# A chunked RWKV-7 recurrence on one core: ScalarE makes the block operand's copy of the state and the modified keys' factor

## The chip, the core and the metric

One NeuronCore of a Trainium2 chip runs the whole program. TensorE (PE in the rows) does the matrix products, VectorE (DVE), ScalarE (ACT) and GpSimd (POOL) work on tiles in on-chip memory, and SyncE (SP) issues the DMAs. Each engine takes its instructions in the order in which they are written for it, and waits on semaphores for the others. The metric is the device time of one execution in microseconds.

## The reference

Two layers of a diffusion trunk are computed for 128 context tokens and 512 latent tokens together (640 rows). A layer is a modulated norm, one projection, four mixers (RWKV-7, latent attention, gMLP, a Fourier mixer) and an output projection. The change lies in the RWKV-7 mixer, which scans the tokens in both directions with a state of 8 heads x 64 x 64:

```python
ah = heads(jax.nn.sigmoid(p['rwkv_a0'][d] + ad @ p['rwkv_a_up'][d]))
kt = kh * (1.0 + (ah - 1.0) * k_a)
...
def step(S, inp):
    r_t, w_t, k_t, v_t, kk_t, a_t = inp
    sa = jnp.einsum('bhvk,bhk->bhv', S, -kk_t)
    S = (S * w_t[:, :, None, :] + sa[..., None] * (kk_t * a_t)[:, :, None, :]
         + v_t[..., None] * k_t[:, :, None, :])
    return S, jnp.einsum('bhvk,bhk->bhv', S, r_t)
```

`kt` are the modified keys; the carried state is S.

## The kernel before, in words

The scan is done in chunks of 64 tokens. A *job* is one chunk in one direction: 2 + 8 chunks times 2 directions, 20 jobs in each of the two layers. `recurrence` holds two generators for a job. `intra` makes everything of a chunk that does not need the carried state: decays (L730 on ScalarE, the scan L732 on VectorE, the exponentials L737 and L739 on ScalarE), the modified keys `kt` (L745, L746), the operands `Ks` and `Qs` (L752 to L757), their products (L765 on TensorE), masked by L768 into `GG`, and then the inverse of a triangular 64 x 64 block by five doubling levels, each a product (L815), a masked copy (L816), two products (L822, L823) and an addition (L826). L831 and L832 follow on TensorE when the last level has been added; L834, L838 and L841 end it. `chain` carries the state through: it copies the state into the block operand `ZZ` (L851, L852), and goes on with L855, L857, L862, L863 and L864, L868, the new state (L870, L871), and the output (L876, L878). Up to four `intra` and two `chain` generators are advanced in turn.

Beside them runs `fill`, dense projections of 128x320 tiles (L168 to L170) that need nothing of the recurrence, evacuated by L355, L374 and L375. Their weights are split by L144 and L145. So TensorE's program is a mixture of small products and groups of six or twelve dense ones.

The order of instructions on an engine is set when the program is built, by a scheduler with costs of its own; taking instructions off an engine may shift others. The two half tiles of `ZZ` (one for each head of a pair, in `HALF[0]` = partitions 0 to 63 and `HALF[1]` = 64 to 127) are filled from the state before L855 and again from R before L868. `p["kah"]` holds half of k_a for each partition, four columns, and `tha` is the tanh from which ah follows as (tha + 1) / 2.

Of the kernel before, what the change touches and what calls it, by code (L numbers as in the profile page):

```python
# [8 lines left out]
F32 = mybir.dt.float32  # L9
F32R = mybir.dt.float32r  # L10
F16 = mybir.dt.float16
AF = mybir.ActivationFunctionType
ALU = mybir.AluOpType
# [43 lines left out]
def trunk(ctx: ExitStack, tc: tile.TileContext, A: dict, O: dict, dbg: dict):  # L57
    nc = tc.nc
    mm = nc.tensor.matmul
    V, S_, G = nc.vector, nc.scalar, nc.gpsimd  # L60

    cst = ctx.enter_context(tc.tile_pool(name="cst", bufs=1))
    lay = ctx.enter_context(tc.tile_pool(name="lay", bufs=2))
# [14 lines left out]
    def bank1():  # L78
        return cur["m"].tile([128, 512], F32, tag="m1", name="m1")
# [136 lines left out]
    def layer_params(l):  # L216
        vec = lay.tile([128, NV], F32, tag="vec", name="vec")
        nc.sync.dma_start(vec, A["vec"][l])

        def g(n):  # L220
            o, c = VEC[n]
            return vec[:, o:o + c]
        p = {n: g(n) for n in VEC}
        d = lay.tile([128, 14 + 14 + 4 + 4 + 32 + 16], F32, tag="der", name="der")
        V.tensor_scalar(d[:, 0:14], p["mu"], -1.0, 1.0, op0=ALU.mult, op1=ALU.add)
        V.tensor_scalar_mul(d[:, 14:28], p["mu"], 0.5)
        V.tensor_scalar_mul(d[:, 28:32], p["kk"], -0.5)
        V.tensor_scalar_mul(d[:, 32:36], p["ka"], 0.5)
        V.tensor_scalar_mul(d[:, 36:68], p["bm"], 0.5)
        V.tensor_scalar_mul(d[:, 68:84], p["wa0"], 0.5)  # L230
        p["omu"], p["hmu"], p["kkn"], p["kah"], p["bmh"], p["wah"] = (
            d[:, 0:14], d[:, 14:28], d[:, 28:32], d[:, 32:36], d[:, 36:68], d[:, 68:84])
        p["mod"] = lay.tile([128, 24, 2], F32, tag="mod", name="mod")
        lp[l] = p
# [109 lines left out]
    def layer(l, X, h, w13):  # L344
        p = lp[l]
# [338 lines left out]
        def recurrence(y):  # L684
            with tc.tile_pool(name=f"rw{l}", bufs=1) as rw:
                units = [(u, j) for u in range(4) for j in range(2)]
                HALF = (slice(0, 64), slice(64, 128))

                def t1k(name, shape=(128, 4, 64), dt=F32):
                    return rw.tile(list(shape), dt, tag="t1", name=name, bufs=8)  # L690

                def keep(name, shape, dt=F32, bufs=3):
                    return rw.tile([128] + list(shape), dt, tag="k" + name, name=name, bufs=bufs)
# [8 lines left out]
                def b3(ps):  # L702
                    return ps[:, 0:256].rearrange("p (a t) -> p a t", t=64)
# [4 lines left out]
                def intra(seg, i, d, A16, XZ):  # L708
# [13 lines left out]
                    def inp(kind):  # L722
                        a = rk[:, 4 * kind:4 * kind + 4, 64 * (ch % 2):64 * (ch % 2) + 64]
                        return a if d == 0 else a[:, :, ::-1]

                    th = th[:, :, 64 * (i % 2):64 * (i % 2) + 64]
                    thw, tha = th[:, 0:4, :], th[:, 4:8, :]
# [14 lines left out]
                    Pi, Pe = P[:, :, 1:65], P[:, :, 0:64]  # L742

                    kt = t1k("kt")
                    V.scalar_tensor_tensor(kt, tha, -1.0, p["kah"][:, 0:4, None].to_broadcast([128, 4, 64]), op0=ALU.add, op1=ALU.mult)  # L745
                    V.scalar_tensor_tensor(kt, kt, 1.0, inp(1), op0=ALU.add, op1=ALU.mult)  # L746
                    yield


# [50 lines left out]
                    for lev in range(1, 6):  # L800
                        if lev == 2:

                            ZZ = keep("ZZ", (2, 4, 64))
# [44 lines left out]

                def chain(it, d, St):
                    Qs, ZZ, GK, GR, Z1, KT, PC, ch, first = it  # L850
                    V.tensor_copy(ZZ[0:64, 0], St[0:64])  # L851
                    S_.copy(ZZ[64:128, 1], St[64:128])  # L852
                    ps = bank1()
                    for u, j in units:
                        mm(ps[HALF[j], 64 * u:64 * u + 64], GK[:, j, u, :], ZZ[:, j, u, :], start=True, stop=True)  # L855
                    R = t1k("R")
                    S_.copy(R, b3(ps))  # L857
                    yield
                    ps = bank1()
                    for u, j in units:  # L860
                        rr = HALF[j]
                        mm(ps[rr, 64 * u:64 * u + 64], Z1[rr, u, :], R[rr, u, :], start=True, stop=True)  # L862
                    V.tensor_copy(ZZ[0:64, 0], b3(ps)[0:64])  # L863
                    S_.copy(ZZ[64:128, 1], b3(ps)[64:128])  # L864
                    yield
                    ps = bank1()
                    for u, j in units:
                        mm(ps[HALF[j], 64 * u:64 * u + 64], KT[:, u, j, :], ZZ[:, j, u, :], start=True, stop=True)  # L868
                    Sn = rw.tile([128, 4, 64], F32, tag="S", name="S", bufs=4)
                    V.tensor_add(Sn, St, b3(ps))  # L870
                    V.tensor_mul(Sn, Sn, PC[:, :, None].to_broadcast([128, 4, 64]))  # L871
                    yield
                    ps = bank1()
                    for u, j in units:
                        rr = HALF[j]
                        mm(ps[rr, 64 * u:64 * u + 64], St[rr, u, :], Qs[rr, u, 1, :], start=(u == 0), stop=False, skip_group_check=True)  # L876
                    for u, j in units:
                        mm(ps[HALF[j], 64 * u:64 * u + 64], ZZ[:, j, u, :], GR[:, j, u, :], start=False, stop=(u == 3), skip_group_check=True)  # L878
                    dst = y[:, :, 64 * ch:64 * ch + 64]
                    if d == 1:  # L880
                        dst = dst[:, :, ::-1]
                    if first:
                        S_.copy(dst, b3(ps))
                    else:
                        V.tensor_add(dst, dst, b3(ps))
                    return Sn
# [6 lines left out]
                while order or active or chains or jobs:  # L893
                    if jobs and len(active) < nact and since >= STAG:
                        jb = jobs.pop(0)
                        active.append((jb, intra(*jb, A16s[count % 3], XZs[count % 3])))
                        count += 1
                        since = 0
                    since += 1

                    if order and len(chains) < 2 and order[0] in done and not any(c[0][0] == order[0][0] and c[0][2] == order[0][2] for c in chains):
                        s_, i, d = jb = order.pop(0)
                        if i == 0:
                            t = rw.tile([128, 4, 64], F32, tag="S", name="S0", bufs=4)
                            if s_ == 0:
                                G.memset(t, 0.0)
                            else:
                                nc.sync.dma_start(t, A["state"][l, :, 4 * d:4 * d + 4, :])
                            state[s_, d] = t
                        chains.append((jb, chain(done.pop(jb), d, state[s_, d])))  # L910
                    running = len(chains) + len(active)
                    for lst in (chains, active):
                        for e in list(lst):
                            try:
# [3 lines left out]
                                s_, i, d = e[0]  # L918
# [341 lines left out]
        if l + 1 < L:  # L1260
            layer_params(l + 1)
# [127 lines left out]
    load_x(X, HALVES[0])  # L1389
    nc.sync.dma_start(con, A["consts"])  # L1390
    layer_params(0)
    V.tensor_copy(c16, i64)
    V.tensor_copy(blk_r, blk)
# [162 lines left out]
```

## Time and profile before

| | |
|---|---|
| median of 3 runs | 2326.18 us (2321.11 to 2326.68) |
| the profiled execution | 2325.5 us, its span 2323.7 us, so 1.8 us lie around the span |
| TensorE busy | 2180.2 us, 94% of the span |
| VectorE busy | 1448.5 us, 62% |
| ScalarE busy | 1103.1 us, 47% |
| GpSimd busy | 890.2 us, 38% |
| mean granted TensorE clock | 0.98 |

Busy shares are means over stages with different limits: the two recurrences (about 370 to 700 us, and 1525 to 1870 us) have to be read by themselves. Times inside the execution are microseconds from the start of the span.

### The profile page before, as it was taken

To read this page: it belongs to the slowest core of one execution; us is meant where nothing else is said; L and a number is where in the kernel's file an instruction comes from. 1 tells how busy PE (TensorE), PEld (TensorE's weight loads), DVE (VectorE), ACT (ScalarE), POOL (GpSimd) and SP (SyncE) were. 2 spreads that over 40 slices of the span, in tenths; PEclk is the share of its full clock that TensorE was granted. 3 is DMA by queue.
4 is the path that set the end of the run, shared out by engine and by line. 5 is a ranking of instruction groups with operands and counts; after the bars stand their busy time and mean duration, and the time that the engine had idled before them with its cause. 6 is when DMAs were issued, how large, how long until landed. Compare 5 with 4: busy or idle time off the path is not lost. (4 is left out here: it accounts for less than half of the span.)

```text
span 2323.7 us, 49631 instructions
## 1 busy us (share of the span) xinstructions
PE 2180.2 (94%) x19662; PEld 2014.1 (87%) x19662; DVE 1448.5 (62%) x2816; ACT 1103.1 (47%) x2399; POOL 890.2 (38%) x892
## 2 busy tenths in 40 slices
PE   6899998999999999899999999989999999998998
PEld 4888897888889999878998888978888899997997
DVE  5677757888874326822366787578889643367225
ACT  5666754444434334423345766544444343344332
POOL 2322125443443335523552222244444334355452
PEclk8999999999999999999999999999999999999999
DMA  7233326332215426565532323362322254264332
GB/s 262 73 100 91 108 88 203 101 91 95 78 58 176 150 74 191 150 226 191 153 96 83 106 80 100 113 198 88 97 87 72 63 178 152 76 187 147 95 106 99
DMA packets 208010, 283.74 MB, mean 122 GB/s; under 512 B 26912, under 2 KB 119712, under 8 KB 207776
## 3 DMA queue, kind: packets, MB, share of 16 engines
q1 hardware_dynamic: 207776, 280.55, 38.8%
q8 instruction: 155, 2.54, 0.5%
q14 instruction: 79, 0.65, 0.1%
HBM read 224.75 MB, written 55.74 MB: 121 GB/s over the span
## 5 line engine op out<-in xcount | busy, mean ns | idle before, releaser
L145 POOL TENSOR_TENSOR wl<-wr,wh 128x512 fp32r<-128x512 f32 x371 | 523.1, 1413 | 966.3 <-ACT wh L144 853.0
L168 PE MATMUL dps<-hhi,wh 128*128 128x320 f32 x2368 | 772.1, 326 | 8.7 <-DVE f L1150 4.2
L169 PE MATMUL dps<-hlo,wh 128*128 128x320 f32 x2368 | 743.6, 314 | 5.9 <-POOL hlo L306 4.6
L170 PE MATMUL dps<-hhi,wl 128*128 128x320 f32 x2368 | 741.3, 313 | 0.0
L168 PEld LDWEIGHTS dps<-hhi,wh 128*128 128x128 f32 x2368 | 452.2, 191 | 23.7 <-DVE f L1150 4.8
L169 PEld LDWEIGHTS dps<-hlo,wh 128*128 128x128 f32 x2368 | 452.6, 191 | 11.8 <-POOL hlo L306 6.6
L170 PEld LDWEIGHTS dps<-hhi,wl 128*128 128x128 f32 x2368 | 451.4, 191 | 0.5
L144 ACT CAST wh<-wr 128x512 fp32r<-128x512 f32 x372 | 229.5, 620 | 304.4 <-PE dps L169 197.1
L168 PE MATMUL dps<-ohi,wh 128*128 128x320 f32 x512 | 161.5, 316 | 1.9 <-ACT wh L144 1.9
L170 PE MATMUL dps<-ohi,wl 128*128 128x320 f32 x512 | 158.9, 311 | 1.0 <-POOL wl L145 1.0
L826 DVE TENSOR_TENSOR XZ<-XZ,m 128x512 f16<-128x512 f16 x200 | 129.5, 677 | 47.7 <-PE m L823 47.4
L169 PE MATMUL dps<-olo,wh 128*128 128x320 f32 x512 | 159.1, 311 | 0.0
L1150 DVE SCALAR_TENSOR_TENSOR f<-f,dps 128x320 f32<-128x320 f32 x96 | 46.2, 485 | 167.7 <-PE dps L170 167.7
L773 POOL TENSOR_TENSOR GG<-GG,con 64x256 f32<-64x256 f32 x80 | 60.7, 759 | 163.2 <-DVE GG L768 160.1
L1144 ACT ACTIVATE f<-dps,der 128x320 f32<-128x320 f32 x128 | 67.2, 525 | 112.7 <-PE dps L170 105.0
L168 PEld LDWEIGHTS dps<-ohi,wh 128*128 128x128 f32 x512 | 97.2, 190 | 10.2 <-issue 5.9
L170 PEld LDWEIGHTS dps<-ohi,wl 128*128 128x128 f32 x512 | 96.7, 189 | 2.4 <-POOL wl L145 1.5
L169 PEld LDWEIGHTS dps<-olo,wh 128*128 128x128 f32 x512 | 96.9, 189 | 1.7 <-issue 1.7
L816 DVE TENSOR_TENSOR T<-m,con 128x256 f16<-128x256 f32 x200 | 80.6, 416 | 18.1 <-PE m L815 17.6
L778 ACT CAST A<-GG 64x256 f16<-64x256 f32 x80 | 32.3, 404 | 90.5 <-POOL GG L773 90.5
L619 DVE TENSOR_TENSOR pl<-m,ph 128x512 fp32r<-128x512 f32 (+1 forms) x96 | 59.1, 619 | 25.0 <-ACT ph L618 23.7
L822 PE MATMUL m<-T,XZ 128*128 128x64 f16 x800 | 66.3, 195 | 5.2 <-DVE T L816 5.2
(496 smaller groups left out, 4627.8 us busy)
## 6 DMA issues: line engine op xcount, KB each, us to landing
wr<-in_w_in SPq DMA_DIRECT2D x180, 256.0 KB, 3.0
wr<-in_w_merge SPq DMA_DIRECT2D x128, 256.0 KB, 2.9
ar<-in_w_ada SPq DMA_DIRECT2D x48, 512.0 KB, 6.3
wr<-in_w_branch SPq DMA_DIRECT2D x64, 256.0 KB, 2.9
zdr<-f SPq DMA_DIRECT2D x48, 320.0 KB, 3.5
rk<-spill SPq DMA_DIRECT2D x20, 768.0 KB, 6.0
thdr<-t SPq DMA_DIRECT2D x32, 320.0 KB, 3.3
odr<-t SPq DMA_DIRECT2D x32, 320.0 KB, 3.6
```

The lines of the kernel that those rows point to most:

```text
L144: S_.copy(hi, src)
L145: (leng or G).tensor_sub(lo, src, hi.bitcast(F32))
L168: mm(ps, hi[:, c], ahi(k)[:, q], start=(k == 0), stop=False)
L169: mm(ps, hi[:, c], alo(k)[:, q], start=False, stop=False)
L170: mm(ps, lo[:, c], ahi(k)[:, q], start=False, stop=(k == K - 1))
L619: V.tensor_sub(pl[:, 0:w], tp[:, 0:w], ph[:, 0:w].bitcast(F32))
L773: G.tensor_sub(GK[HALF[j], j], GK[HALF[j], j], bc(i64[HALF[j]], 4))
L816: V.tensor_mul(T1.rearrange("p u (j k o i) -> p (u j) k o i", j=2, o=2, i=b)[:, :, :, 0, :], ps[:, 0:256].rearrange("p (x k i) -> p x k i" ...
L822: mm(ps[:, 64 * u:64 * u + 64], X1[:, u, :], cols(T1[:, u, :], 0), start=True, stop=True)
L826: V.tensor_add(new, new, ps.rearrange("p (x n i) -> p x n i", x=2, i=b))
L1144: yield from dense(A["w_merge"][l, m, n], 8, H, lambda q, ps: S_.activation(gt[:, q], ps, AF.Tanh, scale=0.5, bias=bias))
L1150: yield from dense(A["w_branch"][l, n, m], 4, (lambda k: o[k][0], lambda k: o[k][1]), lambda q, ps: V.scalar_tensor_tensor(to[:, q], gt[:, ...
```

## The change: what it does

VectorE made `kt` in two instructions: (tha - 1) x kah, and then (that result + 1) x key. Now ScalarE makes the factor 1 + (tha - 1) x kah as kah x tha + (1 - k_a / 2), in four instructions of 64 columns, since scale and bias are one number for each partition and differ between the four column groups; the bias `omk` is made once in a layer. VectorE's second instruction becomes a plain product. And the copy of the state into the first half of `ZZ`, VectorE's L851, is made on ScalarE beside the other half.

```diff
-        d = lay.tile([128, 14 + 14 + 4 + 4 + 32 + 16], F32, tag="der", name="der")
+        d = lay.tile([128, 14 + 14 + 4 + 4 + 32 + 16 + 4], F32, tag="der", name="der")
...
+        V.tensor_scalar(d[:, 84:88], p["ka"], -0.5, 1.0, op0=ALU.mult, op1=ALU.add)
+        p["omk"] = d[:, 84:88]
...
                     kt = t1k("kt")
-                    V.scalar_tensor_tensor(kt, tha, -1.0, p["kah"][:, 0:4, None].to_broadcast([128, 4, 64]), op0=ALU.add, op1=ALU.mult)
-                    V.scalar_tensor_tensor(kt, kt, 1.0, inp(1), op0=ALU.add, op1=ALU.mult)
+                    for u in range(4):
+                        S_.activation(kt[:, u, :], tha[:, u, :], AF.Identity, scale=p["kah"][:, u:u + 1], bias=p["omk"][:, u:u + 1])
+                    V.tensor_mul(kt, kt, inp(1))
                     yield
...
                 def chain(it, d, St):
                     Qs, ZZ, GK, GR, Z1, KT, PC, ch, first = it
-                    V.tensor_copy(ZZ[0:64, 0], St[0:64])
-                    S_.copy(ZZ[64:128, 1], St[64:128])
+                    for j in range(2):
+                        S_.copy(ZZ[HALF[j], j], St[HALF[j]])
```

The lines below the first edit move down by two, those below the second by three: L732 becomes L734, L746 becomes L749, L768 becomes L771, L826 becomes L829. The four new instructions are L748, both copies of the state are L855.

**VectorE, the ninth job of layer 0** (in the trace of before from 492.4 us). `Lc` is the scan, `XZ` the inverse's tile, `GG` the masked products. Before:

```order
L732 SCALAR_TENSOR_TENSOR Lc<-smask,lw 128x256
L745 SCALAR_TENSOR_TENSOR kt<-thl,der 128x256
L863 COPY ZZ<-m_6369 64x256
L826 TENSOR_TENSOR XZ_4243<-XZ_4243,m_6380 128x2x16x16
L826 TENSOR_TENSOR XZ_4244<-XZ_4244,m_6390 128x2x128x2
L746 SCALAR_TENSOR_TENSOR kt<-kt,rk 128x256
L768 TENSOR_TENSOR GG<-m_6401,con 128x512
L768 TENSOR_TENSOR GG<-m_6402,con 128x512
L752 TENSOR_TENSOR Ks<-kt,IP 128x4x64
```

The same place of the changed kernel:

```order
L734 SCALAR_TENSOR_TENSOR Lc<-smask,lw 128x256
L866 COPY ZZ<-m_6398 64x256
L829 TENSOR_TENSOR XZ_4245<-XZ_4245,m_6409 128x2x16x16
L829 TENSOR_TENSOR XZ_4246<-XZ_4246,m_6419 128x2x128x2
L749 TENSOR_TENSOR kt<-kt,rk 128x256
L771 TENSOR_TENSOR GG<-m_6430,con 128x512
L771 TENSOR_TENSOR GG<-m_6431,con 128x512
L755 TENSOR_TENSOR Ks<-kt,IP 128x4x64
```

L745 is gone; the product that needs its successor, L749, stays where L746 stood, ahead of the pair that makes `GG`.

**ScalarE, the same job.** Before:

```order
L730 ACTIVATE lw<-thl,decay 128x256
L737 ACTIVATE P<-Lc 128x4x64
L739 ACTIVATE IP<-Lc 128x256
L864 COPY ZZ<-m_6369 64x256
L144 CAST wh<-wr 128x512
L355 COPY f<-dps 128x320
L778 CAST A_4248<-GG 64x4x64 x2
```

And now:

```order
L732 ACTIVATE lw<-thl,decay 128x256
L739 ACTIVATE P<-Lc 128x4x64
L741 ACTIVATE IP<-Lc 128x256
L748 ACTIVATE kt<-thl,der 128x64
L867 COPY ZZ<-m_6398 64x256
L748 ACTIVATE kt<-thl,der 128x64 x3
L144 CAST wh<-wr 128x512
```

The four new instructions stand behind both exponentials, one ahead of the copy into `ZZ` and three behind it.

**VectorE, the first two jobs of layer 0.** Before:

```order
L732 SCALAR_TENSOR_TENSOR Lc<-smask,lw 128x256
L851 COPY ZZ<-S 64x256
L745 SCALAR_TENSOR_TENSOR kt<-thl,der 128x256
L756 SCALAR_TENSOR_TENSOR Qs<-rk,P 128x4x64
L746 SCALAR_TENSOR_TENSOR kt<-kt,rk 128x256
L752 TENSOR_TENSOR Ks<-kt,IP 128x4x64
L753 SCALAR_TENSOR_TENSOR IP<-thl,IP 128x256
L754 TENSOR_TENSOR Ks<-IP,rk 128x4x64
L732 SCALAR_TENSOR_TENSOR Lc<-smask,lw 128x256
```

And now:

```order
L734 SCALAR_TENSOR_TENSOR Lc<-smask,lw 128x256
L759 SCALAR_TENSOR_TENSOR Qs<-rk,P 128x4x64
L749 TENSOR_TENSOR kt<-kt,rk 128x256
L755 TENSOR_TENSOR Ks<-kt,IP 128x4x64
L734 SCALAR_TENSOR_TENSOR Lc<-smask,lw 128x256
L756 SCALAR_TENSOR_TENSOR IP<-thl,IP 128x256
L757 TENSOR_TENSOR Ks<-IP,rk 128x4x64
```

The second job's scan has moved ahead of the first job's L753 and L754 (now L756 and L757).

## Rows read from the trace of the kernel before

**Rows 1.** Busy time by stretch: us, each engine's busy us (instructions), granted clock, DMA.
```profile
core 0: us, PE busy (x) PEld busy (x) DVE busy (x) ACT busy (x) POOL busy (x), PEclk, DMA share, GB/s
400.00:680.00 280.00, 261.48 (x4120) 230.32 (x4120) 238.08 (x503) 128.03 (x320) 127.58 (x171) 0.99 0.28 89
```

**Rows 2.** Waits of TensorE, whole span: us in total, times, longest.
```profile
PE m L831 <- DVE XZ L826: 30.8, 28, 1.8
```

**Rows 3.** Groups by line on VectorE: busy us, mean ns | idle before.
```profile
L745 DVE SCALAR_TENSOR_TENSOR kt<-thl,der 128x256 f32<-128x256 f32 x40 | 19.3, 482 | 0.1
...
L851 DVE COPY ZZ<-S 64x256 f32<-64x256 f32 x40 | 16.2, 405 | 0.0
```

**Rows 4.** Timeline of VectorE, ninth job: start us, duration us, line.
```profile
493.29 0.40 DVE L745 SCALAR_TENSOR_TENSOR kt<-thl,der 128x256 f32<-128x256 f32 x1
...
493.94 1.26 DVE L826 TENSOR_TENSOR XZ<-XZ,m 128x512 f16<-128x512 f16 x2
495.14 0.41 DVE L746 SCALAR_TENSOR_TENSOR kt<-kt,rk 128x256 f32<-128x256 f32 x1
495.47 1.27 DVE L768 TENSOR_TENSOR GG<-m,con 128x512 f32<-128x512 f32 x2
...
501.53 1.27 DVE L826 TENSOR_TENSOR XZ<-XZ,m 128x512 f16<-128x512 f16 x2
```

**Rows 5.** Timeline of TensorE, L831 of five jobs: wait before it in brackets.
```profile
441.93 0.22 PE L831 MATMUL m<-XZ,A 64*64 64x64 f16 x2 [1.69 <-DVE XZ L826]
...
502.25 0.22 PE L831 MATMUL m<-XZ,A 64*64 64x64 f16 x2 [1.43 <-DVE XZ L826]
...
518.68 0.22 PE L831 MATMUL m<-XZ,A 64*64 64x64 f16 x2 [1.70 <-DVE XZ L826]
...
552.83 0.22 PE L831 MATMUL m<-XZ,A 64*64 64x64 f16 x2 [1.26 <-DVE XZ L826]
...
569.57 0.22 PE L831 MATMUL m<-XZ,A 64*64 64x64 f16 x2 [1.78 <-DVE XZ L826]
```

**Rows 6.** Timeline of ScalarE, ninth job.
```profile
493.46 0.42 ACT L737 ACTIVATE P<-Lc 128x256 f32<-128x256 f32 x1 [1.13 <-DVE Lc L732]
493.79 0.40 ACT L739 ACTIVATE IP<-Lc 128x256 f32<-128x256 f32 x1
494.21 0.37 ACT L864 COPY ZZ<-m 64x256 f32<-64x256 f32 x1
```

**Rows 7.** Timeline of ScalarE at the first norm: instructions with per-partition scale and bias.
```profile
28.79 0.48 ACT L303 ACTIVATE t<-x,mod,s 128x128 f32<-128x128 f32 x1
29.17 0.53 ACT L301 ACTIVATE hhi<-x,mod,s 128x192 fp32r<-128x192 f32 x1
29.61 0.53 ACT L303 ACTIVATE t<-x,mod,s 128x192 f32<-128x192 f32 x1
```

**Rows 8.** Timeline of ScalarE, L739 of two other jobs.
```profile
509.81 0.40 ACT L739 ACTIVATE IP<-Lc 128x256 f32<-128x256 f32 x1
...
652.95 0.40 ACT L739 ACTIVATE IP<-Lc 128x256 f32<-128x256 f32 x1
```

**Rows 9.** Timeline of VectorE, the same two jobs.
```profile
511.14 0.42 DVE L745 SCALAR_TENSOR_TENSOR kt<-thl,der 128x256 f32<-128x256 f32 x1
...
511.93 0.68 DVE L768 TENSOR_TENSOR GG<-m,con 128x512 f32<-128x512 f32 x1
...
654.75 0.68 DVE L768 TENSOR_TENSOR GG<-m,con 128x512 f32<-128x512 f32 x1
```

**Rows 10.** Busy time in stretches of 2 us, columns as in Rows 1.
```profile
570.00:572.00 2.00, 1.84 (x14) 1.86 (x14) 0.98 (x4) 0.93 (x3) 0.05 (x1) 0.67 0.44 95
572.00:574.00 2.00, 2.00 (x28) 1.65 (x27) 0.21 (x1) 0.55 (x2) 0.00 (x0) 0.50 0.10 36
```

**Rows 11.** Timeline of VectorE, start of the recurrence of layer 0.
```profile
382.62 1.59 DVE L732 TENSOR_TENSOR_SCAN Lc<-smask,lw 128x256 f32<-128x256 f32 x1 [0.88 <-ACT lw L730]
...
391.54 1.41 DVE L745 SCALAR_TENSOR_TENSOR kt<-thl,der 128x256 f32<-128x256 f32 x1
```

**Rows 12.** Timeline of TensorE, its first product of the recurrence.
```profile
381.94 2.50 PE L765 MATMUL m<-Qs,Ks 64*128 64x128 f32 x16 [5.00 <-DMA ZZ<-vtok]
```

## Prediction

> **What bounds the kernel now.** I read the share of each engine first, then the busy time by stretch, the waits of TensorE, and the timelines of VectorE, ScalarE and TensorE around one job of the recurrence. Over the span TensorE looks like the only bound. In the steady part of the recurrence that is not the whole of it: of 280 us TensorE is busy 261.48, VectorE 238.08, and ScalarE only 128.03 [rows 1]. The two busy engines take turns. TensorE never runs out of instructions, but it stops at one place: before L831, which needs the second addition L826 of the inverse, 28 times and 30.8 us in all [rows 2]; the recurrence has 40 jobs, so that is nearly every job. One job, the ninth, shows why. VectorE adds the pair L826 at 493.94, makes `kt` (L746) at 495.14 and the masked pair L768 at 495.47, and then works without a gap until it comes to the next pair L826 at 501.53 [rows 4]. TensorE has done its own work by then and has waited 1.43 us when L831 starts at 502.25 [rows 5]. From L831 to the next products L822 and L823 TensorE sets the pace, with the dense products in its program. So a job has a stretch that VectorE bounds (from one pair L826 to the next, through L768) and a stretch that TensorE bounds. Only what changes the first of them, by up to the waits in [rows 2], moves the end; work of VectorE that lies in the second is covered by TensorE's.
>
> **What it removes.** L745 and L851, 40 of each, are 19.3 + 16.2 = 35.5 us of VectorE [rows 3]. Where L851 stands behind the second pair L826, or L745 ahead of the first one, it lies in TensorE's stretch: the ninth job has L745 at 493.29, ahead of the pair [rows 4], and nothing waits for it there. By the two orders, of the 15 steady jobs of a layer three have L745 between the pair L826 and L768, as at 511.14 [rows 9]; a step from such an instruction to the next is 0.33 us (495.14 to 495.47) [rows 4]. Three have L851 in the stretch, two of them among the seven below.
>
> **What it adds, and where.** ScalarE gets four instructions with two per-partition operands on 64 columns. Such instructions take 0.48 us on 128 columns and 0.53 on 192, start to start 0.38 and 0.44 [rows 7]; 64 columns fewer than 128 are 0.43 us each at a step of 0.33. The bounds are 0.38 (the step at 128 columns) and 0.17 (the step of 0.33 between L737 and L739 on 256 columns without such operands [rows 6], less 192 columns at the 0.06 per 64 of [rows 7]). I take 0.33, since the rows of 128 and 192 columns have the same operands.
> The Trainium skill's "ScalarE: Activation LUTs", section "What ACT_TABLE_LOAD costs", gives 186 ns, 93 ns for each per-partition operand, and 0.833 ns a column, with 93 ns of overlap: 425 ns at a step of 332 ns as an estimate from that page. The row agrees, and the sum by the one and the other is the same.
>
> In the ninth job these four stand behind L737 and L739, which wait for the scan L732, though they don't need it. L739 starts at 493.79 [rows 6]. The first new one starts 0.33 later, at 494.12, and ends at 494.55. The copy L864 follows; in the trace it began only when L739 had ended (494.21 against 493.79 + 0.40 [rows 6]), so I let it run alone, 494.57 to 494.94. The other three start at 494.96, 495.29 and 495.62, and the last ends at 496.05. VectorE, in order, reaches the product of `kt` when its pair L826 ends at 495.20 (493.94 + 1.26) and has to wait there for some 0.8 us; behind it stands L768, whose products are ready, then `Ks`, the state's L870 and L871, and the next pair L826 for which TensorE waits. The product starts at 496.08, L768 at 496.41 instead of 495.47: 0.94 us later. In short, L768 comes 2.60 to 2.62 us after L739's start.
>
> By the orders, the 15 steady jobs fall into four kinds. Seven are like the ninth; the last of them has L739 at 652.95 and L768 at 654.75 [rows 8, 9], so L768 would come at 655.55, 0.80 later. Their mean is about 0.8, 5.7 us for the seven. Off go 0.6 for L851 in two of them, and 0.9 for two in which TensorE did not wait for L831 at all and has some slack: 4.2 us. Three are like the job of 511.14: L739 at 509.81 puts L768 at 512.42 instead of 511.93 [rows 8, 9], 0.5 later although L745 is gone: 1.5 us. In three the product stands behind L768, so the wait is covered; they gain L745's 0.33, but only one has a wait of TensorE to give up: -0.3. Two stay as they are. In the job ahead of these fifteen two instructions leave the stretch: -0.5. The sum is 4.9 us a layer, 10 us in all.
>
> **What follows from longer waits.** TensorE's granted clock falls to 0.50, its level of 1.2 GHz instead of 2.4, in 572 to 574 us, after the wait of 1.78 us that ended at 569.57, and is 0.67 in the stretch before [rows 5, 10]. The 4 us lose 0.33 x 2 + 0.50 x 2 = 1.7 us of full speed, in the part that TensorE bounds. The waits of 1.70 and 1.69 us [rows 5] are at the edge. Waits of 1.43 and 1.26 us [rows 5] become 2.4 and 1.7. I count three such falls more in the two layers together: 5 us, with bounds of none and 10.
>
> **The start of each recurrence.** VectorE has no idle time there, and loses L745, one of them 1.41 us long [rows 11]. Against it, the first job's L753 and L754 now stand behind the second job's scan, which started at 382.62 because it waited for its input [rows 11]; so TensorE's first L765, at 381.94 before [rows 12], comes at about 385, and the product of `kt` waits for ScalarE there too. Most of it is caught up as L745 is missing later. I take -1 us a layer, with bounds of -4 and +3. The one small instruction for the bias in a layer, and the second copy of the state on ScalarE, cost nothing: ScalarE has half of its time free [rows 1], and the copy's user L855 comes after a whole group of dense products. Without that cover the copy costs its own 0.4.
>
> **Sum.** 2325.5 + 10 + 5 - 2 = 2338.5 us for the profiled execution; the median of the runs stands 0.7 above it, so 2339.
>
> **The rivals.**
> *Relief wins (faster).* The wait for ScalarE is covered, and VectorE's stretch becomes shorter. For it: VectorE is busy 85% of the steady part, ScalarE 46% [rows 1]. If the last of the four ended before the second L826 does, the three L745, three L851 and the job ahead of the fifteen would give 0.33 x 3 + 0.31 x 3 + 0.5 = 2.4 us a layer, the start 1 to 4, and one fall of the clock less in each 1.7: about 5 us a layer, 2316. It is decided in the seven jobs: the four must be 0.85 us earlier than I have them. Against it: the step that this needs is 0.12 us (0.33 - 0.85 / 4), below my lower bound.
> The Trainium skill's "Perfetto Trace Analysis", section "Optimizing Scalar/DVE Operations", says that with VectorE saturated it may make sense to move work to ScalarE. By that rule this is the case to expect. Here the row on busy shares is for it, the order of the rows at the ninth job against.
> *Wait and relief cancel (no change).* With a step of 0.17 the last of the four ends 0.6 us earlier; the seven jobs lose 0.2 each, the three of the second kind gain 0.1, L851 gives 0.9, the falls of the clock stay as they are, and the start gives 1: about 2325.
> *ScalarE becomes late for all (slower still).* If the copies into `ZZ` for L855 or the evacuations of dense products queue behind the new work, TensorE waits there as well: half a microsecond in each of 36 jobs is 18 us more, 2355. Against it: its busy time rises by 4 x 0.33 + 0.4 = 1.7 us a job, some 30 us on 128 in 280.
>
> **How the numbers follow.** My forecast has 0.57, no change 0.23, relief 0.15, the late ScalarE 0.05. A difference under 0.3%, 7 us, is about what a measurement of this kernel can't tell from none. Faster is the relief, 0.15; slower is the forecast and the late ScalarE, less a little for the forecast's lower end, 0.60; the rest, 0.25, is the same. The likeliest case alone runs from 2331 to 2348 (its bounds for the clock and the start). The range for 8 in 10 takes in the no-change case and most of the relief, and the lower part of the late case: 2318 to 2350.
>
> **What would show it.** Right: VectorE idle before L749 for 0.3 to 0.9 us in ten jobs a layer, released by ScalarE's L748; the wait of TensorE before L831 (now L834) up from 30.8 to about 40 us; more stretches at half clock; VectorE's busy time down by some 35 us all the same. Wrong: L748 at a smaller step than 0.33, or the product of `kt` released by the pair ahead of it; then the time would be at or under 2326. For the start: TensorE's first L765 about 3 us after its 381.94, with the jobs of the steady part some 1 us ahead of where they stood.

## The result, and the profile after

The changed kernel takes 2350.99 us (median of 4 runs, 2346.97 to 2356.88), before takes 2325.22 (4 runs, 2321.11 to 2326.68). The ratio is 1.0116, 95% interval [1.0101, 1.013]: 25.8 us slower, where 13 were forecast and the range ended at 2350. The profiled execution is the slowest of the four, 2356.88 us.

The page's first part, busy us of each engine:
```profile
PE 2190.5 (93%) x19662; PEld 2021.8 (86%) x19662; DVE 1429.9 (61%) x2738; ACT 1176.0 (50%) x2599; POOL 885.6 (38%) x892
```
The span grew by 31.4 us, from 2323.7 to 2355.1. TensorE is busy 10.3 us longer with the same 19662 instructions, at a mean granted clock of 0.975 where it was 0.980; the other 21.1 us are idle time. The stretch of [rows 1] again:
```profile
400.00:680.00 280.00, 251.82 (x3894) 221.50 (x3891) 226.41 (x450) 154.46 (x392) 122.11 (x167) 0.98 0.27 87
```
VectorE is busy less and ScalarE more, as meant, and TensorE gets 226 fewer instructions done in the same 280 us. Two of TensorE's waits in the whole span:
```profile
PE m L834 <- DVE XZ L829: 36.2, 30, 2.5
PE m L825 <- DVE T L819: 15.1, 30, 2.2
```
The first was 30.8 us [rows 2]. The second, for the masked copy `T` of a doubling level (L816, now L819), was 5.2 us in 10 waits before. What releases VectorE ahead of the keys' product, by that line's instructions:
```profile
L749 DVE TENSOR_TENSOR kt<-kt,rk x40: 409/426/887, 382.7 to 1835.7; 128x256 f32<-128x256 f32 x40
...
its engine sat idle before it (us, times) until:
  ACT kt L748: 21.6, 25
```
Before there was nothing like it: the factor was VectorE's own. The ninth job, VectorE's timeline, beside [rows 4]:
```profile
497.51 1.28 DVE L829 TENSOR_TENSOR XZ<-XZ,m 128x512 f16<-128x512 f16 x2
499.78 0.42 DVE L749 TENSOR_TENSOR kt<-kt,rk 128x256 f32<-128x256 f32 x1 [0.99 <-ACT kt L748]
500.12 1.28 DVE L771 TENSOR_TENSOR GG<-m,con 128x512 f32<-128x512 f32 x2
...
504.24 0.89 DVE L756 SCALAR_TENSOR_TENSOR IP<-thl,IP 128x256 f32<-128x256 f32 x1
...
506.19 1.27 DVE L829 TENSOR_TENSOR XZ<-XZ,m 128x512 f16<-128x512 f16 x2
```
The masked pair starts 2.61 us after the pair L829 (500.12 - 497.51) where it was 1.53 (495.47 - 493.94), so 1.08 later. ScalarE meanwhile, beside [rows 6]:
```profile
497.49 0.40 ACT L741 ACTIVATE IP<-Lc 128x256 f32<-128x256 f32 x1
497.80 0.42 ACT L748 ACTIVATE kt<-thl,der 128x64 f32<-128x64 f32 x1
498.25 0.37 ACT L867 COPY ZZ<-m 64x256 f32<-64x256 f32 x1
498.64 1.10 ACT L748 ACTIVATE kt<-thl,der 128x64 f32<-128x64 f32 x3
```
That is the queue of the prediction, to 0.1 us: one activation, the copy alone, three activations at a step of 0.34 us ((1.10 - 0.42) / 2). TensorE's waits before the first L834 of three jobs:
```profile
506.92 0.22 PE L834 MATMUL m<-XZ,A 64*64 64x64 f16 x2 [2.29 <-DVE XZ L829]
...
525.32 0.27 PE L834 MATMUL m<-XZ,A 64*64 64x64 f16 x2 [2.21 <-DVE XZ L829]
...
578.18 0.22 PE L834 MATMUL m<-XZ,A 64*64 64x64 f16 x2 [2.40 <-DVE XZ L829]
```
Behind two of them, stretches of 2 us; the clock (the third number from the end) is at 1.2 GHz, half of its upper level:
```profile
509.00:511.00 2.00, 2.00 (x28) 1.65 (x27) 0.23 (x1) 0.82 (x3) 0.00 (x0) 0.50 0.00 0
...
580.00:582.00 2.00, 2.00 (x28) 1.64 (x27) 0.11 (x1) 1.05 (x3) 0.00 (x0) 0.50 0.32 120
```

### The profile page after: what moved, and what is told of

It reads as the page before. It is cut to its first block, busy times and chain, and to the rows that moved or that the text cites. A ratio compares the mean times of both kernels' runs of the same rounds, so it can differ in the third digit from the quotient of the medians.

```text
span 2355.1 us, 49767 instructions
## 1 busy us (share of the span) xinstructions
PE 2190.5 (93%) x19662; PEld 2021.8 (86%) x19662; DVE 1429.9 (61%) x2738; ACT 1176.0 (50%) x2599; POOL 885.6 (38%) x892
## 5 line engine op out<-in xcount | busy, mean ns | idle before, releaser
L829 DVE TENSOR_TENSOR XZ<-XZ,m 128x512 f16<-128x512 f16 x200 | 129.7, 678 | 49.8 <-PE m L826 49.8
L819 DVE TENSOR_TENSOR T<-m,con 128x256 f16<-128x256 f32 x200 | 80.6, 416 | 20.7 <-PE m L818 20.0
L825 PE MATMUL m<-T,XZ 128*128 128x64 f16 x800 | 68.8, 195 | 15.3 <-DVE T L819 15.1
```

Source lines behind the costliest of these rows:

```text
L819: V.tensor_mul(T1.rearrange("p u (j k o i) -> p (u j) k o i", j=2, o=2, i=b)[:, :, :, 0, :], ps[:, 0:256].rearrange("p (x k i) -> p x k i" ...
L825: mm(ps[:, 64 * u:64 * u + 64], X1[:, u, :], cols(T1[:, u, :], 0), start=True, stop=True)
L829: V.tensor_add(new, new, ps.rearrange("p (x n i) -> p x n i", x=2, i=b))
```

## The experiments

The theory: VectorE waits in order for ScalarE's late factor, ahead of the masked pair, and TensorE waits for what the pair holds back. Rivals: ScalarE's load, the copy's latency, the shifted orders. All ratios are to before in the same series of runs, with 95% intervals; before's median lay between 2319.87 and 2325.22 us in the six series, so ratios are compared here, and a difference of ratios is given in us by multiplying it by 2325.

**The two parts apart.** `zz_only` has the copy alone (and no `omk`), `kt_only` the factor alone:
```
zz_only, against the changed kernel
-                    for u in range(4):
-                        S_.activation(kt[:, u, :], tha[:, u, :], AF.Identity, scale=p["kah"][:, u:u + 1], bias=p["omk"][:, u:u + 1])
-                    V.tensor_mul(kt, kt, inp(1))
+                    V.scalar_tensor_tensor(kt, tha, -1.0, p["kah"][:, 0:4, None].to_broadcast([128, 4, 64]), op0=ALU.add, op1=ALU.mult)
+                    V.scalar_tensor_tensor(kt, kt, 1.0, inp(1), op0=ALU.add, op1=ALU.mult)
kt_only, against the changed kernel
-                    for j in range(2):
-                        S_.copy(ZZ[HALF[j], j], St[HALF[j]])
+                    V.tensor_copy(ZZ[0:64, 0], St[0:64])
+                    S_.copy(ZZ[64:128, 1], St[64:128])
```


> Before with one edit alone: both halves of the block operand's copy of the state on ScalarE, VectorE keeps the keys' factor; the orders of the engines are those of before but for that copy. Theory of the late factor (VectorE waits at the keys' product for ScalarE's four activations, which stand behind the exponentials, and holds back the masked pair, so TensorE): no such wait is here, 2320 to 2326 us, no idle time before the keys' product. Rival, the copy's latency (the state's copy now ends a ScalarE step later in each of 40 chain steps, and the chain sets the end): 2335 to 2350, most of the loss.

> The changed kernel with the state's copy back on VectorE; the four activations for the keys' factor stay on ScalarE. Theory of the late factor: the whole loss is here, 2346 to 2354 us, with 20 to 24 us of VectorE's idle time before the keys' product. Rival, the copy's latency: 2325 to 2335.

`zz_only`: 2313.77 us, 0.9958 [0.9946, 0.9971]. `kt_only`: 2354.38 us, 1.0132 [1.0117, 1.0147]. The copy is a gain, larger than either theory said, and the factor more than the whole loss, with 22.0 us of idle time before the product. The copy's latency is out. In `zz_only` TensorE's wait, 30.8 us before, is:
```profile
PE m L831 <- DVE XZ L826: 25.8, 26, 1.8
```

**ScalarE's load.** `load_idle` is `zz_only` with four activations in the change's place on ScalarE, whose results nobody reads; VectorE's order stays in the steady part and shifts a little in the start. (`issue_after` gives the place in an engine's queue, behind the named instruction, and waits for nothing; `ex` is the second exponential, `pairs[-1]` and `sums[-1]` below are the last masked pair and the last L874 issued.)
```
...
+                    with tc.issue_after(ex.ins):
+                        for u in range(4):
+                            S_.activation(k2, tha[:, u, :], AF.Identity, scale=p["kah"][:, u:u + 1], bias=p["kah"][:, u:u + 1])
```


> The kernel with the copy alone on ScalarE, and four activations of 128x64 more in each job in the place where the change has them, behind the exponentials, whose results nobody reads; VectorE makes the factor as before, and its order is that of the copy alone. Theory of the late factor: the load by itself costs little, 2313 to 2319 us. Rival, ScalarE's load: 2330 to 2350, most of the 40 us between the copy alone and the factor alone.

2315.39 us, 0.9961 [0.9949, 0.9973], the same as `zz_only`. The load costs nothing that can be measured.

**The wait taken away.** `prod_behind` is the changed kernel with one instruction queued elsewhere on VectorE:
```
+                    with tc.issue_after(pairs[-1].ins) if pairs else ExitStack():
                         V.tensor_mul(kt, kt, inp(1))
...
```


> The changed kernel with the keys' product queued on VectorE behind the masked pair of the job ahead, so that the late factor no longer holds the pair back; ScalarE's order stays. Theory of the late factor: no idle time before the keys' product worth speaking of (below 5 us in all), and the time at that of the copy alone less a little, 2308 to 2320 us. Rival, ScalarE's load of 1.7 us a job: 2335 to 2350. Rival, a longer string on VectorE between the pair and the next level step (the wait at TensorE's level products grows from 5 to 15 us in the changed kernel and stays): 2325 to 2335.

2314.43 us, 0.9956 [0.9942, 0.997]. Queueing this one product elsewhere gives back 37 us (0.0160 x 2325) of the changed kernel's time; `Ks`, which needs it, goes behind the pair with it wherever it stood ahead. The product's group (busy us, mean ns | idle before):
```profile
L750 DVE TENSOR_TENSOR kt<-kt,rk 128x256 f32<-128x256 f32 x40 | 22.5, 563 | 2.3 <-ACT kt L748 2.3
```
The ninth job on VectorE: the masked pair (now L772) follows the addition at once, 1.31 us after its start.
```profile
490.89 1.27 DVE L831 TENSOR_TENSOR XZ<-XZ,m 128x512 f16<-128x512 f16 x2
492.20 1.29 DVE L772 TENSOR_TENSOR GG<-m,con 128x512 f32<-128x512 f32 x2
493.41 0.58 DVE L750 TENSOR_TENSOR kt<-kt,rk 128x256 f32<-128x256 f32 x1
```
ScalarE's last three activations, in the same place as in the changed kernel, end at 493.12, under the cover of the pair:
```profile
492.02 1.10 ACT L748 ACTIVATE kt<-thl,der 128x64 f32<-128x64 f32 x3
```
So where the product, and `Ks` with it, stands in VectorE's queue decides, not how much ScalarE does. `only_behind` is the same without the copy on ScalarE.

> The factor on ScalarE alone, the state's copy on VectorE as before, and the keys' product queued behind the masked pair. Theory of the late factor: the 2354 us of the factor alone fall to 2318 to 2326, about those of before, since without the wait the factor's move gains and loses little. Rival, that the copy on ScalarE is what makes the move bearable: 2330 to 2345.

2312.74 us, 0.9962 [0.9947, 0.9976]; its expectation was too high. `mid_behind` is `prod_behind` with the loop of the four moved to just behind L732, ahead of the exponentials.

> As the one before, and the four activations between the decay's activation and the first exponential, where ScalarE otherwise waits 0.6 us for the scan. Theory of the late factor: as the one before within 5 us, 2308 to 2320, the exponentials about 1.1 us later but used only behind the pair. Rival, late exponentials (the keys' other product and the masked pair of the next job wait for them): 2325 to 2340.

2317.35 us, 0.997 [0.9958, 0.9982], in the range of the theory.

**Earlier or fewer activations.** `kt_early` has the loop of the four moved ahead of `S_.activation(lw...)`, L732; `one_act` replaces it:
```
-                    for u in range(4):
-                        S_.activation(kt[:, u, :], tha[:, u, :], AF.Identity, scale=p["kah"][:, u:u + 1], bias=p["omk"][:, u:u + 1])
+                    S_.activation(kt, tha, AF.Identity, scale=p["kah"][:, 0:1], bias=p["omk"][:, 0:1])
```


> The changed kernel with the four activations ahead of the decay's activation instead of behind the exponentials, so that the factor is there long before VectorE multiplies it; ScalarE has the same work. The scan then stands behind VectorE's level step instead of ahead of it. Theory of the late factor: no idle time before the keys' product, and the time back to 2312 to 2328 us. Rival, ScalarE's load (1.7 us more in each of 40 jobs, whatever its place): 2340 to 2352, as the changed kernel.

> The changed kernel with one activation of 128x256 in the place of the four of 128x64 (it takes the first column group's factor and offset for all four groups, so the keys of the other three are not the reference's). It ends about 1.3 us sooner. Theory of the late factor: the wait shrinks from 0.9 to below 0.2 us a job, 2318 to 2332 us. Rival, the orders that the change gave the engines (the level step's product ahead of the state's sum in some jobs): these orders are here too, so 2340 or more.

`kt_early`: 2332.24 us, 1.0035 [1.0023, 1.0048]. `one_act`: 2335.45 us, 1.0052 [1.0038, 1.0065]. Both lie between the theories. The product's wait is nearly gone in `one_act` and half gone in `kt_early`:
```profile
L748 DVE TENSOR_TENSOR kt<-kt,rk 128x256 f32<-128x256 f32 x40 | 19.4, 484 | 2.4 <-ACT kt L747 2.3
```
```profile
L749 DVE TENSOR_TENSOR kt<-kt,rk 128x256 f32<-128x256 f32 x40 | 20.2, 506 | 10.1 <-ACT kt L733 10.0
```
But the orders shifted: in `one_act` the keys' first product `Ks`, in `kt_early` the scan `Lc`, now stands between the addition and the masked pair, and in `one_act` TensorE waits 12.5 us for `T`:
```profile
PE m L824 <- DVE T L818: 12.5, 27, 1.5
```
`one_ks` is `one_act` with that `Ks` queued behind the pair.

> The kernel with one activation of 128x256 in the place of four (first group's factor for all, so its keys are not the reference's), which took 2335 us, with the keys' first product queued behind the masked pair instead of ahead of it. Theory (whatever delays the masked pair costs): the 21 us that this kernel lay above the copy alone were that product of 0.4 us and its wait for the exponential, ahead of the pair: 2306 to 2316 us. Rival, the other shifts of the orders: 2328 to 2336.

2310.27 us, 0.9958 [0.9943, 0.9972]. That `Ks` ahead of the pair, with what the scheduler shifted beside it, was the whole difference of 22 us (0.0094 x 2325), and TensorE's wait for `T` went from 12.5 to 4.2 us. `mid_ks` is the full computation in this form: four activations ahead of the exponentials, the product ahead of the pair, `Ks` behind it.

> The changed kernel with the four activations between the decay's activation and the first exponential, the keys' product left ahead of the masked pair (its factor is now there in time), and only the keys' first product with the exponential queued behind the pair. Theory of the late factor: no wait ahead of the pair, and VectorE's string is short of the 0.41 us that the copy-alone kernel has there, so 2304 to 2314 us, as without the factor (2304.6). Rival: the exponentials are late by the four activations, 2316 to 2325.

2311.67 us, 0.9965 [0.9954, 0.9977]. The loss is gone, and the time lies in the expected range; but by its ratio it is not as fast as `no_factor2` below (0.9921), as the theory had it.

**The price of the wait, in doses.** `two_ks` and `three_ks` are `one_ks` with two activations (`for u in (0, 2)`, on `u:u + 2`) and three; `four_clean` has all four, and is the changed kernel with `Ks` behind the pair and with L801, a masked copy that opens the inverse and waits for ScalarE's cast, behind the new state's L874. Its order on VectorE is near that of the other three, but in three steady jobs of a layer the product stands behind the pair, where `three_ks` has it ahead. `sum_first` has only the last of these edits:
```
+                    with tc.issue_after(sums[-1].ins) if sums else ExitStack():
                         V.tensor_mul(X1, A16, bc(m1T, 4))
...
```


> The changed kernel's order on VectorE with two activations of 128x128 in the place of the four of 128x64 (one group's factor for two groups, so its keys are not the reference's): about 0.85 us sooner than four. With one it took 0.9958 of before, with four 1.0116. If the loss goes as the wait at the keys' product, and the wait as what is left of the lateness (0.09 us a job in 25 with one, 0.86 with four), 0.998 to 1.003 of before with 0.2 to 0.4 us a wait. Rival, a threshold (TensorE's clock falls only with the longest waits): 0.995 to 0.997.

> As the one before with three activations (one of 128x128, two of 128x64; two groups share a factor): 1.003 to 1.008 of before if the loss goes as the wait, with 0.5 to 0.7 us a wait. Rival, a threshold: 0.997 to 1.002.

> The changed kernel with one shift of its order on VectorE taken back: in three jobs of each layer the level step's first product (it waits for ScalarE's cast) stands behind the state's sum and the next level step again, as before, instead of ahead of them. If this shift makes the 10 us by which TensorE's waits for the level step grew, and what they do to its clock, 1.003 to 1.008 of before, and those waits fall from 15 to about 6 us. If the wait at the keys' product makes the whole loss, 1.010 to 1.013, the same as the changed kernel.

> As the one before, and the keys' first product behind the masked pair also in the two jobs of each layer that had it ahead: all four activations, on the order of the kernels with one to three. Loss in proportion to the lateness: 1.006 to 1.010 of before, three activations having taken 1.0045. Rival (the shifts are harmless): as the changed kernel, 1.010 to 1.013.

The product's group in `two_ks`, `three_ks` and `four_clean`, one each:
```profile
L749 DVE TENSOR_TENSOR kt<-kt,rk 128x256 f32<-128x256 f32 x40 | 18.4, 460 | 10.5 <-ACT kt L748 10.2
```
```profile
L749 DVE TENSOR_TENSOR kt<-kt,rk 128x256 f32<-128x256 f32 x40 | 18.0, 451 | 19.6 <-ACT kt L748 19.6
```
```profile
L749 DVE TENSOR_TENSOR kt<-kt,rk 128x256 f32<-128x256 f32 x40 | 19.0, 474 | 21.0 <-ACT kt L748 21.0
```
| kernel | wait for the factor, us | ratio |
|---|---|---|
| `one_ks` | 2.3 | 0.9958 [0.9943, 0.9972] |
| `two_ks` | 10.2 | 1.0008 [0.9996, 1.002] |
| `three_ks` | 19.6 | 1.0045 [1.003, 1.0061] |
| `four_clean` | 21.0 | 1.0038 [1.0024, 1.0051] |
| `sum_first` | 21.5 | 1.0096 [1.008, 1.0112] |
| changed kernel | 21.6 | 1.0116 [1.0101, 1.013] |

From one activation to three the loss goes as the wait: 20 us of time (0.0087 x 2325) for 17.3 us of waiting. The middle dose lies near the line between them (1.0008, where the line has 0.9998), so nothing here points to a threshold. The line would put `four_clean` at 1.0052; it came lower, 1.0038, under its expectation of 1.006 to 1.010 too, and the three products behind the pair may be why. The changed kernel has 0.6 us more of waiting at the product than `four_clean`, but 18 us more of time (0.0078 x 2325): that is what the order of the other instructions costs. The `Ks` ahead of the pair, in two steady jobs of a layer and at its start, is 13.5 us of it (1.0096 - 1.0038), in the profiles about half in the start and half in the steady part; L801, in three jobs of a layer, is 4.6 (1.0116 - 1.0096), with intervals that overlap. The expectation of `sum_first` gave L801 more: 1.003 to 1.008, and TensorE's wait for `T` down from 15.1 to about 6 us. It fell to 11.2, and to 7.6 in `four_clean`.

**What a VectorE instruction is worth.** `no_factor2` is `zz_only` without L745 (the keys get another factor) and with `Ks` and L753 behind the pair; `factor_twice` is `zz_only` with L745 issued twice; `before_behind` and `zz_behind` are before and `zz_only` with L746 behind the pair, by the same `issue_after` as above.
```
no_factor2, against zz_only
-                    V.scalar_tensor_tensor(kt, tha, -1.0, p["kah"][:, 0:4, None].to_broadcast([128, 4, 64]), op0=ALU.add, op1=ALU.mult)
-                    V.scalar_tensor_tensor(kt, kt, 1.0, inp(1), op0=ALU.add, op1=ALU.mult)
+                    V.scalar_tensor_tensor(kt, tha, 1.0, inp(1), op0=ALU.add, op1=ALU.mult)
...
```

> The kernel with the copy alone on ScalarE, and VectorE's instruction that makes the keys' factor left out (the keys are multiplied by the raw gate plus one, so the result is not the reference's); nothing is added on ScalarE, and the keys' first product stays behind the masked pair. It tells what the relief of VectorE is worth when nothing has to be waited for. Theory of the late factor: the instruction stood under a wait of VectorE for ScalarE's exponentials or for TensorE in most jobs, so 2305 to 2314 us. Rival, VectorE's string sets the pace (0.41 us a job in all 40 jobs): 2295 to 2303.

> The kernel with the copy alone on ScalarE, and VectorE's instruction for the keys' factor issued twice with the same result: 0.41 us more ahead of the masked pair in each of 40 jobs, and no new wait for ScalarE. Theory (whatever delays the masked pair costs): one of these taken away gave 9 us, so one more costs 9 to 20, 2323 to 2334 us. Rival, only waits cost, and the string has room: 2313 to 2318.

> Before, with nothing moved to ScalarE and only the keys' second instruction queued on VectorE behind the masked pair of the job ahead. If the gain of the last kernels over before (0.9956 to 0.9965) comes from this place alone, 0.995 to 0.998 of before; if it needs the moves to ScalarE, 0.999 to 1.002.

> The copy alone on ScalarE and the keys' second instruction queued behind the masked pair. If the copy's gain (0.9958) and the place's add up, 0.991 to 0.994 of before; if both take away the same delay of TensorE, 0.995 to 0.997.

`no_factor2`: 2304.61 us, 0.9921 [0.9909, 0.9932]. `factor_twice`: 2309.49, 0.9953 [0.994, 0.9966], so an instruction more cost nothing, against the expectation: in most steady jobs L746 had moved behind the pair, and the pair stood as far behind the addition as in `zz_only` (1.53 us). `before_behind`: 2316.41, 0.9967 [0.9954, 0.998]. `zz_behind`: 2312.15, 0.9945 [0.9931, 0.996], the fastest version that computes the reference, though its interval overlaps that of `zz_only`; the copy's gain and the place's do not fully add up. With the product in that place, the factor's move to ScalarE is worth nothing clear: 0.9962 (`only_behind`) against 0.9967, and with the copy 0.9956 (`prod_behind`) against 0.9945. The gain of those kernels is the place's and the copy's. In these runs what stands between the addition and the masked pair is paid for, what stands behind the pair hardly.

## Why the prediction was wrong in size

**What it removes: undersized.** The copy was counted in three of fifteen jobs, at about 0.3 us each. Alone it gives 9.8 us. From the first L831 of a job to that of the next, `zz_only` is shorter than before in four jobs of layer 0 and the same within 0.2 us in the others: 17.3 to 16.1, 18.1 to 15.8, 16.1 to 14.9, 16.2 to 14.8. The falls of the clock at 519 and 571 us are gone there, though one has come at 395; so part of the relief works through the clock. In the two profiled executions the steady parts of both layers are 13.5 us shorter, and the clock lost in them fell from 10.2 to 1.7. Without any wait, L745 left out gives 9 us more (0.9958 to 0.9921), less what `Ks` and L753 behind the pair give.

**What it adds: right.** The step, the queue on ScalarE, the wait at the product in the ninth job (0.99 us measured, 0.8 forecast) and the delay of the pair (1.08 against 0.94) all came. The lower bound for the step is 0.15 by its own terms (0.33 - 3 x 0.06), not 0.17; with 0.34 measured, nothing hangs on it.

**Where: the count failed.** The step that failed is the sum over the kinds of jobs, 4.9 us a layer. The steady part (first L831 of a layer to its last, L834 after) went from 291.6 to 304.0 us and from 294.2 to 305.2, 23.4 us in all, against 10 and the clock's 5. From the start of the last addition to that of the masked pair, the two kinds of jobs that the sum has as late came out near it: the seven by 6.8 us a layer (5.7 forecast), the three by 1.5 (1.5). Two terms were wrong. The two jobs that were to stay as they are have the pair 0.54 us later each: in before the keys' product stood ahead of the addition and only `Ks` between, now both stand between.
```profile
527.35 0.43 DVE L746 SCALAR_TENSOR_TENSOR kt<-kt,rk 128x256 f32<-128x256 f32 x1
...
528.02 1.27 DVE L826 TENSOR_TENSOR XZ<-XZ,m 128x512 f16<-128x512 f16 x2
529.22 0.41 DVE L752 TENSOR_TENSOR Ks<-kt,IP 128x256 f32<-128x256 f32 x1
529.55 1.27 DVE L768 TENSOR_TENSOR GG<-m,con 128x512 f32<-128x512 f32 x2
```
```profile
534.51 1.27 DVE L829 TENSOR_TENSOR XZ<-XZ,m 128x512 f16<-128x512 f16 x2
535.77 0.43 DVE L749 TENSOR_TENSOR kt<-kt,rk 128x256 f32<-128x256 f32 x1
536.24 0.42 DVE L755 TENSOR_TENSOR Ks<-kt,IP 128x256 f32<-128x256 f32 x1
536.58 1.28 DVE L771 TENSOR_TENSOR GG<-m,con 128x512 f32<-128x512 f32 x2
```
And the job ahead of the fifteen, put at -0.5, has the pair 0.89 later, since the product came ahead of it there and waits for ScalarE (before, then after):
```profile
417.04 1.27 DVE L826 TENSOR_TENSOR XZ<-XZ,m 128x512 f16<-128x512 f16 x2
...
418.57 1.28 DVE L768 TENSOR_TENSOR GG<-m,con 128x512 f32<-128x512 f32 x2
```
```profile
420.09 1.26 DVE L829 TENSOR_TENSOR XZ<-XZ,m 128x512 f16<-128x512 f16 x2
...
422.16 0.43 DVE L749 TENSOR_TENSOR kt<-kt,rk 128x256 f32<-128x256 f32 x1 [0.81 <-ACT kt L748]
422.51 1.28 DVE L771 TENSOR_TENSOR GG<-m,con 128x512 f32<-128x512 f32 x2
```
In all the pair is late by 10.3 us a layer in 13 jobs, where the forecast had 6.7 (5.7 + 1.5 - 0.5) before it took off for cover. Two things more lay outside the sum. L801 now stands ahead of the new state's instructions in two more jobs of a layer, and TensorE got a second place to wait (L825, 15.1 us). And VectorE's later instructions grew longer (last section); no run gives the price of that.

**The clock: right in the steady part.** In stretches of 2 us, time times what is missing from full clock, the steady parts lost 10.2 us before and 15.3 after, 5.1 more: the forecast was 5. That is one execution of each; `kt_only`, of about the same time as the changed kernel, lost 22.1, so the closeness may be luck. What one fall costs is seen in the third job of the two layers before. In layer 0 it has none, from 441.93 [rows 5] to 457.12, 15.19 us; in layer 1, 16.63:
```profile
457.12 0.22 PE L831 MATMUL m<-XZ,A 64*64 64x64 f16 x2 [0.35 <-DVE XZ L826]
...
1593.93 0.22 PE L831 MATMUL m<-XZ,A 64*64 64x64 f16 x2 [1.68 <-DVE XZ L826]
...
1610.56 0.22 PE L831 MATMUL m<-XZ,A 64*64 64x64 f16 x2 [0.34 <-DVE XZ L826]
```
```profile
1596.00:1598.00 2.00, 2.00 (x21) 1.65 (x21) 0.00 (x0) 1.77 (x6) 0.23 (x1) 0.50 0.00 0
```
So a fall cost 1.4 us there, a little under the 1.7 that I took.

**The start: wrong sign.** From the first activation of L730 to the first L831 it was 34.1 us in both layers, and is 34.8 and 39.5: 6.1 more, not 2 less. TensorE's first product of the recurrence came at 387.36 instead of 381.94, 3.5 us later after the 1.9 that had built up before the recurrence; that much the prediction had, but it was not caught up. The lost clock there doubled, from 6.8 to 13.7 us. `four_clean` has 34.2 and 34.6, `prod_behind` 32.7 and 33.8: in the changed kernel's start, too, the order around the pair is what cost.

**The sum with measured terms:** -10.2 us for what is removed without the wait (`prod_behind`, 0.9956), +19.1 for the wait (to `four_clean`), +13.5 for `Ks` and +4.6 for L801, together +27.0, which is 1.0116. As steps from one run to the next they add up by construction. The 19.1 hold the product's place ahead of the pair too, but `one_ks` has that place with hardly a wait, and 0.9958. The 10.2 hold the place's gain: `before_behind` has 7.7 of them without any move. All but `Ks` and L801 come to +8.9 us, less than the 13 forecast; what carried the time past the range is the 18.1 for these two, which the prediction had at nothing. The rival "relief wins" had a true half: the copy alone gained 9.8 us. For the factor the place in the queue turned it round. The Trainium skill's "Perfetto Trace Analysis", section "Optimizing Scalar/DVE Operations", says that where VectorE is saturated, offloading some work to ScalarE may make sense; the runs agree for the copy (0.9958) and disagree for the factor as it was placed (1.0132). "Late for all" came to nearly the measured time, but by another way: the activations that nobody reads cost nothing.

Still open: how much of the copy's gain is the clock's beyond those two executions, why its gain and that of the product's place add up only in part, and how `Ks` in two steady jobs and the start comes to 13.5 us.

## What to carry to other kernels

When work goes from a busy engine to a free one, look at the instruction that takes the result back, and at what is queued behind it: one product that came 0.9 us late in 25 jobs cost more than the whole relief, and queued behind its neighbour it cost nothing, though the factor's move then gained nothing clear either. Read the whole order between the two points that bound a stretch, not only the pair in question, since a scheduler that gets new work shifts others into it too. Before work is moved at all, try the order alone: without any move it gave 0.33% here.

## What the runs showed of the hardware

Some of VectorE's instructions took longer beside GpSimd's. L756 takes 0.42 us in the changed kernel's steady parts where GpSimd is idle throughout, and where it works for over nine tenths of L756's time, 0.85 to 1.83, in all 14 cases. Six more, with GpSimd at work for 0.85 to 0.87 of the time, took only 0.41 to 0.56, so the overlap alone does not set it. The 0.89 of the ninth job above lies beside this instruction of GpSimd's:
```profile
503.99 1.66 POOL L783 TENSOR_TENSOR Alo<-GG,A 64x256 f16<-64x256 f32 x2
```
The mean of L756 (L753 before) went from 652 to 834 ns, that of L759 (L756 before) from 619 to 751, and VectorE's total fell by 18.6 us where 35.5 were taken off [rows 3]. The Trainium skill's "GPSIMD Engine Reference", section "1. Specifications", says that GpSimd shares its way to SBUF with VectorE, and that VectorE's instructions with two inputs in SBUF contend there; L756 has two, and the trace agrees in the 14 cases. This was read from the traces alone; no run took GpSimd's work away.
